# Moving each output store ahead of the round's second load, and ending the hand-written section behind the last store instead of ahead of it

## The chip, the cores and the metric

The kernel runs on one core of one Trainium2 chip. The metric is device time in microseconds (us) of one execution. Before the change the median of three executions is 262.35 us (262.20 to 262.47).

## The reference

For each of 16 batches it multiplies the transpose of a 768 x 512 matrix by a 768 x 1024 matrix, all float32 in memory:

```python
batch, m, k, n = 16, 512, 768, 1024
x: (batch, k, m)   y: (batch, k, n)
np.einsum('bkm,bkn->bmn', x, y).astype(np.float32)
```

So x(b) is 1.5 MB, y(b) 3 MB and the result of a batch 2 MB. Loads and stores together are 109 MB.

## The kernel before

One batch is one round. Everything is written inside one hand-written section (`tc.tile_critical()`, lines 45 and 46): each engine gets a fixed list of instructions, and all waits between engines are semaphores set by hand. The scheduler of the Tile layer orders nothing in it.

- **SP** issues all transfers, on one queue. Lines 102 to 111 are its main loop: for batch b the load of x(b) into `xs[b % 2]` (line 106), the load of y(b) into `ys[b % 2]` (line 109), and, from b = 4 on (`LAG = 4`), the store of the batch four rounds back, `store(b - 4)` (lines 110 and 111, 93 to 100). Below, s(b) is the store of batch b. Ahead of x(b) SP waits until x(b-2) has been cast, and ahead of y(b) until y(b-2) has been cast, because the two float32 buffers of each input are reused every second round. Ahead of s(b), for b below 14, it waits for the `groups` semaphore to reach 2(b+2), which means that TensorE has ended batch b+1; by then ScalarE must have copied batch b out. s(14) waits for `outs`, which ScalarE raises behind its copy of batch 14. After the loop come s(12), s(13) and s(14) (lines 112 and 113).
- **VectorE** casts x(b) and y(b) to bf16, into `xb` and `yb`, two buffers each (lines 118 to 128). Before batch b it waits until TensorE has ended batch b-2. The cast of y(15) alone is cut in two halves.
- **GpSimd** turns finished casts into the semaphore `ready` for TensorE (lines 131 to 134).
- **TensorE** runs 48 matmuls a batch in two groups of 24 (lines 139 to 155); each group fills one half of PSUM and raises `groups`.
- **ScalarE** copies each group from PSUM to one of five output buffers `ob[b % 5]` (lines 161 to 172). Before batch b it waits until s(b-5) has landed.

The end: SP waits until s(11), s(12) and s(13) have landed (lines 174 and 175), and the section is closed (line 176). Closing has a step in which SP signals the four other engines, each answers, and SP waits for all answers. Behind it, in the hands of Tile, stands s(15) (line 181); Tile makes the end of the program wait for its landing and ends with barriers over all engines (they carry the line of the launch, 207).

All transfers lie on one queue, q1, and each is spread over 16 DMA engines; a DMA's semaphore gets 16 landing events, one from each. The order on the queue before the change, in the middle of the run, is x(b), y(b), s(b-4), x(b+1), y(b+1), s(b-3), and so on. At the end it is x(15), y(15), s(11), s(12), s(13), s(14), s(15).

Of the kernel before, what the change touches and what calls it, by code (L numbers as in the profile page):

```python
# [1 line left out]

_os.environ.setdefault("NEURON_RT_ULTRASERVER_MODE", "4")

# [2 lines left out]

# [5 lines left out]


@with_exitstack
def kernel(
    ctx: ExitStack,
    tc: tile.TileContext,
    x: bass.AP,
    y: bass.AP,  # L20
    out: bass.AP,
):
    nc = tc.nc
    P = 128
    FP32 = mybir.dt.float32
    BF16 = mybir.dt.bfloat16

    B, K, M = x.shape
    _, _, N = y.shape
    KT = K // P  # L30
    MT = M // P
    NF = 512
    NT = N // NF

    x_v = x.rearrange("b (p ko) m -> b p ko m", ko=KT)
    y_v = y.rearrange("b (p ko) n -> b p ko n", ko=KT)
    o_v = out.rearrange("b (p mo) n -> b p mo n", mo=MT)

    LAG = 4
    NO = 5
    KH = KT // 2

    section = ExitStack()
    section.enter_context(tc.tile_critical())
    ec = ctx.enter_context
    xs = [ec(nc.sbuf_tensor(f"xs{i}", [P, KT, M], FP32)) for i in range(2)]
    ys = [ec(nc.sbuf_tensor(f"ys{i}", [P, KT, N], FP32)) for i in range(2)]
    xb = ec(nc.sbuf_tensor("xb", [P, 2, KT, M], BF16))  # L50
    yb = ec(nc.sbuf_tensor("yb", [P, 2, KT, N], BF16))
    ob = [ec(nc.sbuf_tensor(f"ob{i}", [P, MT, N], FP32)) for i in range(NO)]

    HB = MT // 2
    ps = [ec(nc.psum_tensor(f"ps{i}", [P, HB, NT, NF], FP32)) for i in range(2)]
    sx = [ec(nc.semaphore(f"sx{i}")) for i in range(2)]
    sy = [ec(nc.semaphore(f"sy{i}")) for i in range(2)]
    so = [ec(nc.semaphore(f"so{i}")) for i in range(NO)]
    cast = ec(nc.semaphore("cast"))
    ready = ec(nc.semaphore("ready"))  # L60
    room = ec(nc.semaphore("room"))
    groups = ec(nc.semaphore("groups"))
    idle = ec(nc.semaphore("idle"))
    outs = ec(nc.semaphore("outs"))


    made = {}

    def wide_dma(key, dst, src, dram_rows, load):


        if key not in made:
            made[key] = nc.sync.dma_start(dst, src)
            return made[key]
        pat = mybir.BassSymbolicTensorAccessPattern
        widen = lambda a: a.rearrange("(q r) k m -> q (r k m)", r=dram_rows)
        plain = lambda a: a.rearrange("p k m -> p (k m)")
        s, d = (widen(src), plain(dst)) if load else (plain(src), widen(dst))
        return nc.sync.add_instruction(_copy.replace(
            made[key].ins, name=nc.get_next_instruction_name(),  # L80
            ins=(pat(ap=s.ap, dtype=s.dtype, bass_ap=s, is_dma=False),),
            outs=(pat(ap=d.ap, dtype=d.dtype, bass_ap=d, is_dma=False),),
            sync_info=None, ant_dge_precooked=False))


    def parts(b):
        return 2 if b in (15,) else 1


    nx = [sum(1 + parts(a) for a in range(b)) + 1 for b in range(B)]  # L90


    def store(b):


        if b < B - 2:
            nc.sync.wait_ge(groups, 2 * (b + 2))
        else:
            nc.sync.wait_ge(outs, b - (B - 3))
        nc.sync.dma_start(o_v[b], ob[b % NO][:]).then_inc(so[b % NO], 16)  # L100

    for b in range(B):
        i = b % 2
        if b >= 2:
            nc.sync.wait_ge(cast, nx[b - 2])
        wide_dma("x", xs[i][:], x_v[b], 4, True).then_inc(sx[i], 16)
        if b >= 2:
            nc.sync.wait_ge(cast, nx[b - 2] + parts(b - 2))
        wide_dma("y", ys[i][:], y_v[b], 2, True).then_inc(sy[i], 16)
        if b >= LAG:  # L110
            store(b - LAG)
    for b in range(B - LAG, B - 1):
        store(b)


    for _ in range(60):
        nc.vector.sem_inc(idle, 1)
    for b in range(B):
        i = b % 2
        n = 16 * (b // 2 + 1)  # L120
        if b >= 2:
            nc.vector.wait_ge(groups, 2 * (b - 1))
        nc.vector.wait_ge(sx[i], n)
        nc.vector.tensor_copy(xb[:, i], xs[i][:]).then_inc(cast, 1)  # L124
        nc.vector.wait_ge(sy[i], n)
        for h in range(parts(b)):
            ks = slice(h * KT // parts(b), (h + 1) * KT // parts(b))
            nc.vector.tensor_copy(yb[:, i, ks], ys[i][:, ks]).then_inc(cast, 1)  # L128


    for b in range(B):
        nc.gpsimd.wait_ge(cast, nx[b]).then_inc(ready, 1)
        for h in range(parts(b)):
            nc.gpsimd.wait_ge(cast, nx[b] + h + 1).then_inc(ready, 2 // parts(b))


    x_w = xb[:].rearrange("p s k (j mo) -> p s k mo j", mo=MT)
    pe = OrderedEngineSet([nc.tensor.engine])
    with nc.Fori(0, B // 2, engines=pe):
        with nc.Fori(0, 2, engines=pe) as s:  # L140
            nc.tensor.wait_ge(ready, 2).then_inc(ready, -2)
            for mo in range(MT):
                g, m = divmod(mo, HB)
                if m == 0:
                    nc.tensor.wait_ge(room, 1).then_inc(room, -1)  # L145
                for kt in range(KT):
                    if mo == 0 and kt == KH:
                        nc.tensor.wait_ge(ready, 1).then_inc(ready, -1)
                    for nt in range(NT):
                        mm = nc.tensor.matmul(  # L150
                            ps[g][:, m, nt], x_w[:, bass.ds(s, 1), kt, mo],
                            yb[:, bass.ds(s, 1), kt, nt * NF:(nt + 1) * NF],
                            start=(kt == 0), stop=(kt == KT - 1))
                if m == HB - 1:
                    mm.then_inc(groups, 1)


    nc.scalar.nop().then_inc(room, 2)
    for _ in range(60):
        nc.scalar.sem_inc(idle, 1)  # L160
    for b in range(B):
        if b >= NO:
            nc.scalar.wait_ge(so[b % NO], 16 * (b // NO))
        for g in range(2):
            nc.scalar.wait_ge(groups, 2 * b + g + 1)
            cp = nc.scalar.copy(ob[b % NO][:, g * HB:(g + 1) * HB].rearrange("p m (t f) -> p m t f", f=NF),  # L166
                                ps[g][:])
            if b < B - 1:
                cp.then_inc(room, 1)
        if b == B - 2:  # L170
            nc.scalar.drain().then_inc(outs, 1)
    cp.then_inc(outs, 1)

    for b in range(B - LAG - 1, B - 2):
        nc.sync.wait_ge(so[b % NO], 16 * (b // NO + 1))
    section.close()

    nc.sync.dma_start(o_v[B - 1], ob[(B - 1) % NO][:])


# [1 line left out]
_INS = ['x', 'y']  # L185
_OUTS = [((16, 512, 1024), 'float32')]


# [23 lines left out]
```

## Time and profile before

| what | value |
|---|---|
| median of three executions | 262.35 us |
| the profiled execution, its own time | 262.47 us |
| its span in the profile | 260.7 us |
| busy: TensorE matmul / VectorE / ScalarE | 186.1 / 82.0 / 61.1 us |
| read from and written to HBM | 75.50 MB, 33.55 MB |
| load of x: count, size, median issue to landing | 16, 1536 KB, 29.7 us |
| load of y | 16, 3072 KB, 28.2 us |
| store | 16, 2048 KB, 32.6 us |

The span runs from the first to the last instruction that the profile counts; the execution's own time is 1.8 us longer. "Landing" is the time from the issue of a DMA to its last landing event, so a transfer that stands long in the queue has a long one. In the views of waits, "SPq" is the instruction stream of SP. In the timelines the columns are: start, duration (both us), engine, line, operation, output and input, count, and in brackets how long the engine had been idle and what ended that.

### The profile page before, as it was taken

How to read it: one execution, taken by the hardware profiler on the slowest of the kernel's cores; microseconds unless marked ns; L12 is line 12 of the kernel's file. 1: busy time of each engine (PE TensorE's matmuls, PEld its weight loads, DVE VectorE, ACT ScalarE, POOL GpSimd, SP SyncE). 2: the span in 40 equal slices, each digit the busy share in tenths (PEclk: the TensorE clock that was granted, in tenths of full speed). 3: DMA queues.
4: the chain of work that ended last, by engine and by line, in shares of the span. 5: the costliest groups of instructions: out<-in, count | busy, mean ns of one | idle time of the engine just before them, and what ended most of it. 6: DMA issues, size and time to landing. Idle time of an engine off the chain costs nothing. (4 is left out here: it accounts for less than half of the span.)

```text
span 260.7 us, 2506 instructions
## 1 busy us (share of the span) xinstructions
PE 186.1 (71%) x768; PEld 89.8 (34%) x768; DVE 82.0 (31%) x33; ACT 61.1 (23%) x33; POOL 0.2 (0%) x4
## 2 busy tenths in 40 slices
PE   0009999998937949479596894969959197696910
PEld 0004555554512515124242351434425043253500
DVE  0261644525222252312524115252142522225000
ACT  1000442243220222202214022040322205022220
POOL 0000000000000000000000000000000000000000
PEclk9999999999995999959889797797999889799985
DMA  7998999999899899989999989999998999999994
GB/s 260 432 494 385 468 385 468 392 392 488 385 410 493 370 450 475 427 385 405 483 400 437 465 367 453 410 483 402 410 485 382 445 468 417 410 410 430 427 410 181
DMA packets 4514, 109.07 MB, mean 418 GB/s; under 512 B 768, under 2 KB 768, under 8 KB 768
## 3 DMA queue, kind: packets, MB, share of 16 engines
q1 hardware_dynamic: 4512, 109.05, 98.1%
q14 instruction: 2, 0.02, 0.0%
HBM read 75.50 MB, written 33.55 MB: 418 GB/s over the span
## 5 line engine op out<-in xcount | busy, mean ns | idle before, releaser
L150 PE MATMUL ps<-yb,xb 128*128 x768 | 186.1, 407 | 62.7 <-PEq L145 60.7
L150 PEld LDWEIGHTS ps<-yb,xb 128*128 x768 | 89.8, 117 | 158.5 <-issue 92.2
L166 ACT COPY ob<-ps 128x2048 f32<-128x2048 f32 x32 | 59.8, 1870 | 184.2 <-PE ps L150 184.2
L128 DVE CAST yb<-ys 128x6144 bf16<-128x6144 f32 (+1 forms) x17 | 53.8, 3171 | 87.7 <-DMA ys<-in_y_dram 87.7
L124 DVE CAST xb<-xs 128x3072 bf16<-128x3072 f32 x16 | 28.2, 1760 | 69.4 <-DMA xs<-in_x_dram 65.3
L166 ACT ACT_TABLE_LOAD x1 | 1.3, 1283 | 5.3 <-issue 5.3
L196 POOL MEMSET const-bfloat16-1.0<- 128x1 bf16 x1 | 0.1, 102 | 0.0
L196 POOL MEMSET const-uint8-127<- 128x1 uint8 x1 | 0.1, 102 | 0.0
L196 POOL MEMSET const-float32-1.0<- 128x1 f32 x1 | 0.1, 99 | 0.0
L196 POOL MEMSET const-float32-0.0<- 128x1 f32 x1 | 0.1, 98 | 0.2 <-issue 0.2
## 6 DMA issues: line engine op xcount, KB each, us to landing
ys<-in_y_dram SPq DMA_DIRECT2D x16, 3072.0 KB, 28.2
out_dram<-ob SPq DMA_DIRECT2D x16, 2048.0 KB, 32.6
xs<-in_x_dram SPq DMA_DIRECT2D x16, 1536.0 KB, 29.7
```

The costliest lines, as they stand in the source:

```text
L124: nc.vector.tensor_copy(xb[:, i], xs[i][:]).then_inc(cast, 1)
L128: nc.vector.tensor_copy(yb[:, i, ks], ys[i][:, ks]).then_inc(cast, 1)
L150: mm = nc.tensor.matmul(ps[g][:, m, nt], x_w[:, bass.ds(s, 1), kt, mo], yb[:, bass.ds(s, 1), kt, nt * NF:(nt + 1) * NF], start=(kt == 0), ...
L166: cp = nc.scalar.copy(ob[b % NO][:, g * HB:(g + 1) * HB].rearrange("p m (t f) -> p m t f", f=NF), ps[g][:])
L196: nc = _bacc.Bacc("TRN2", target_bir_lowering=False, num_devices=1)
```

## The change

Two things are edited; the computation, the transfers' sizes and the buffers stay as they are.

1. For b = 4 to 14 the store s(b-4) is issued between x(b) and y(b), and no longer behind y(b). For b = 15 it stays behind y(15). The loop behind issues s(12) to s(15), s(15) with a wait for `outs` to reach 2, which ScalarE raises with its last copy.
2. The section is entered for the whole function, so that it ends when the function returns. s(15) is inside it, and SP waits inside it for all stores (the five `so` semaphores). Tile issues nothing behind it.

```diff
-    section = ExitStack()
-    section.enter_context(tc.tile_critical())
+    ctx.enter_context(tc.tile_critical())
...
         wide_dma("x", xs[i][:], x_v[b], 4, True).then_inc(sx[i], 16)
+        if LAG <= b < B - 1:
+            store(b - LAG)
         if b >= 2:
             nc.sync.wait_ge(cast, nx[b - 2] + parts(b - 2))
         wide_dma("y", ys[i][:], y_v[b], 2, True).then_inc(sy[i], 16)
-        if b >= LAG:
+        if b == B - 1:
             store(b - LAG)
-    for b in range(B - LAG, B - 1):
+    for b in range(B - LAG, B):
         store(b)
...
-    for b in range(B - LAG - 1, B - 2):
-        nc.sync.wait_ge(so[b % NO], 16 * (b // NO + 1))
-    section.close()
-
-
-
-
-    nc.sync.dma_start(o_v[B - 1], ob[(B - 1) % NO][:])
+    for i in range(NO):
+        nc.sync.wait_ge(so[i], 16 * len(range(i, B, NO)))
```

## The prediction

> **What bounds the kernel now.** I read the DMA rows of the page first.
>
> ```profile
> DMA  7998999999899899989999989999998999999994
> ...
> q1 hardware_dynamic: 4512, 109.05, 98.1%
> ...
> HBM read 75.50 MB, written 33.55 MB: 418 GB/s over the span
> ```
>
> The first row is the busy share of the 16 DMA engines in 40 slices: close to full from the second slice to the last but one. The queue is busy for 98.1% of the span, while TensorE has 71%. The transfers are the bound. Next comes the question whether the queue ever runs dry, which the instruction streams answer. This is one round of the timeline (140 to 176 us).
>
> ```profile
> 140.69 3.36 DVE L128 CAST yb<-ys 128x6144 bf16<-128x6144 f32 x1 [5.45 <-DMA ys<-in_y_dram]
> 140.99 1.87 ACT L166 COPY ob<-ps 128x2048 f32<-128x2048 f32 x1 [3.25 <-PE ps L150]
> 144.08 0.47 SPq L73 DMA_DIRECT2D ys<-in_y_dram  x1
> ...
> 144.58 12.23 PE L150 MATMUL ps<-yb,xb 128*128 x48 [3.63 <-PEq L145]
> 144.59 0.58 SPq L100 DMA_DIRECT2D out_dram<-ob  x1
> ...
> 149.28 1.76 DVE L124 CAST xb<-xs 128x3072 bf16<-128x3072 f32 x1 [5.23 <-DMA xs<-in_x_dram]
> ...
> 151.07 0.47 SPq L73 DMA_DIRECT2D xs<-in_x_dram  x1
> ```
>
> y(9) has landed and is cast at 140.69 to 144.05; then SP issues y(11), and s(7) half a microsecond later; after the cast of x(10) it issues x(12). VectorE and TensorE sit idle until data land, and the page's median landing times are 28 to 33 us for transfers that take 4 to 7 us each. So some 24 us of work stands in the queue at any time. Last, the end:
>
> ```profile
> 219.89 3.36 DVE L128 CAST yb<-ys 128x6144 bf16<-128x6144 f32 x1 [5.46 <-DMA ys<-in_y_dram]
> 223.82 12.24 PE L150 MATMUL ps<-yb,xb 128*128 x48 [4.01 <-PEq L145]
> 235.70 3.43 DVE L128 CAST yb<-ys 128x3072 bf16<-128x3072 f32 x2 [5.46 <-DMA ys<-in_y_dram]
> 238.03 10.72 PE L150 MATMUL ps<-yb,xb 128*128 x48 [1.97 <-ACT ob L166]
> 248.79 1.87 ACT L166 COPY ob<-ps 128x2048 f32<-128x2048 f32 x1 [3.26 <-PE ps L150]
> 250.88 0.33 SPq L181 DMA_DIRECT2D out_dram<-ob  x1
> ```
>
> Batch 14 is cast at 219.89 and multiplied from 223.82, batch 15 from 238.03; its copy ends at 250.66 and s(15) is issued at 250.88. The landing events in the trace show who is last: the 16 engines end s(14) between 251.56 and 255.09, and s(15) between 256.97 and 259.90. One engine lags, and its steps from store to store are 4.85, 4.84, 4.85, 4.81 us for s(12) to s(15): no gap. **The end is this one engine's total of bytes**, not the compute chain: it took s(15) up at 255.09, 4.2 us after the issue.
>
> **The change, part by part.**
>
> *The moved stores, SP's side.* Eleven stores (s(0) to s(10)) change places with eleven loads; no DMA is added. s(b-4) waits until TensorE has ended batch b-3. For b = 11 that is batch 8, at 140.95; x(11) was issued at 135.27, y(11) at 144.08. So the store can go at 141.0, before y(11) may be issued anyway (cast of y(9) ends at 144.05). Behind the waiting store stands y(b), then x(b+1). If TensorE is late, y(b) is late too, but its turn on the queue comes some 20 us after its issue, which hides any such delay. I cost SP's side at nothing; without that cover it would be the store's issue, about 0.5 us a round.
>
> *The moved stores, the queue's side.* On the lagging engine a load of x takes 3.66 us, of y 7.28, a store 4.86: 15.8 a round in either order. y(4) to y(14) land 4.86 us later and the store 7.28 earlier; x stays. All are needed later than they land but y, and a later y moves VectorE and TensorE alike by 4.9 us. Steady state: y lands, 3.4 us cast, 0.5 to the first matmul, 10.5 to 13.5 of matmuls, within 15.8. Nothing ends on this before the tail, so 0.
>
> *The queue's losses at transitions.* 16 times 15.8 is 252.8 us; from the first packet at 1.98 that gives 254.8, and the lagging engine ends at 259.90. Of the 5.1 us lost, 2.2 are the first two loads (5.26 and 7.93 us); 2.4 are four loads, y(4), y(5), y(6) and y(8), with steps of 7.84, 8.01, 7.93 and 7.76 instead of 7.28. In the packet records the late packets are those that stand last before a store: 1.82 us normally, up to 2.63 there. Before a load they are not late. After the change the last packet of x stands before the store, of the same 49152 bytes, and the number of such transitions is 12 as before (s(11) still follows y(15)). The trace doesn't show x before a store: the bounds are that all these losses go (2.5 us less) and that each of the 12 transitions costs the largest excess seen, 0.8 us (9.7 less 2.5, 7 us more). I take 0, since packet, size and count are the same and the steps after y(10) show hardly any loss.
>
> *The tail, compute.* y(14) now lands at 224.73, when s(10) landed before, and not at 219.87. Its matmuls start 3.95 us after that, at 228.68; with 12.24 us they end at 240.92. Batch 15 waits for them instead of for its data (ready at 237.6), and back to back a batch takes 10.36 (starts of 31.36 and 41.72 in the early part, where TensorE runs without idle time). That gives 251.28, the copy ends at 253.2, and s(15) is issued at about 253.25 instead of 250.88. Before, the middle engine landed s(15) 6.2 us after its issue (257.08 less 250.88), so now at 259.45. The lagging engine starts s(15) at 255.09 in either case and ends at 259.90. So it still ends last, by 0.45 us: cost 0, cover 0.45 us. A DMA's fixed cost as the Trainium skill gives it bears on this: "DMA: Bandwidth & Descriptors", section "Anatomy of one DMA — SWDGE (gpsimd) path", puts it at about 2.0 us plus bytes over 436 GB/s, though for another way of issuing than this kernel's. An estimate from that page is 6.8 us for a store, so landing at 260.05 and 0.15 us lost; the trace's 6.2 us decides here.
>
> *The end of the section.* Before, its closing lies ahead of s(15): by the records SP sees s(13) landed at 250.25, signals at 250.48, the engines answer to 250.70, SP has all answers at 250.79 and issues s(15) at 250.88. That is 0.63 us, beside the lagging engine's transfer of s(13) and s(14), so it cost nothing. After the last landing (259.90) came 0.07 us of SP's wait and then the final barriers to 260.70. Now the same closing comes behind the last landing, with nothing beside it, and then the same final barriers: **+0.63, less about 0.05** for Tile's own wait for s(15), which goes. The nearest row is the closing itself, so I take 0.58. The bounds are 0.3 (the signal at 250.48 to the issue, if the 0.23 before it is not repeated) and 0.8 (two more semaphores to be waited for).
>
> *Sum:* 0 + 0 + 0 + 0 + 0.58. The profiled execution has 262.47, which becomes 263.05. It lies 0.12 above the median of the runs shown, so I forecast 262.35 + 0.6 = **262.95 us**, 0.23% slower. About 0.2%, or 0.5 us, is what a measurement of this kernel can tell from no change.
>
> **The rivals.**
>
> *The compute tail ends last.* If TensorE's first matmuls of batch 14 run at the half clock for longer, s(15) comes too late to be hidden. For it: of the batches from 5 on, two took 13.51 and 13.37 us instead of 12.24, with a granted clock of 0.5 for 6.8 us. That is 1.2 more, less the cover of 0.45: 0.75 more, 263.7. It decides once s(15) is issued later than 253.7. Against: the batches 4, 6 and 12 took 10.55. Chance 0.20, 263.1 to 264.0.
>
> *Fewer losses at the transitions, so faster.* If what makes the last packet late is tied to y (its 24 KB for each partition, or the moment in the round at which it lands), an x before the store is spared. Price: 2.5 us on the lagging engine at most, from y(4), y(5), y(6), y(8) and y(10); with the 0.6 of the end, 260.45; at half, 261.7. It decides when more than 0.6 of the 2.5 goes. For it: seven of the twelve transitions cost nearly nothing, so the loss depends on something. Against: x packets are as large. Chance 0.22, 260.4 to 262.6.
>
> *More losses at the transitions.* Casts of y now run when x's last packets land, which they didn't. One to two us more on top of 0.6: 264 to 265. Chance 0.08.
>
> *It doesn't do what it says.* The closing could overlap the last landings, or the landing of the lagging engine could vary by that much: 262.2 to 262.7, chance 0.05.
>
> **How the numbers follow.** The forecast, 262.6 to 263.3 with the bounds of the closing, has 0.45; of that 0.30 lie above 262.87 (0.2%) and 0.15 below. Slower: 0.30 + 0.20 + 0.08 = 0.58. Faster: 0.17 of the second rival's 0.22. Within 0.2%: 0.15 + 0.05 + 0.05 = 0.25. The range 261.3 to 264.0 leaves out the far half of the faster rival (0.08) and most of the third (0.06).
>
> **What would show it.** Right: q1's busy time (98.1% of 260.7, 255.7 us) is the same; the last landing stays within 0.4 us of 259.9; the time from it to the end of the span grows from 0.8 to 1.4 us; s(15) is issued near 253.3; TensorE starts batch 15 without idle time. Wrong: a last landing earlier by a microsecond with fewer late packets (second rival), a last landing 6.2 us behind the issue of s(15) (first rival), or slices with the DMA below 9 in the middle, which would mean that the queue does run dry.

## The result

The changed kernel takes 263.20 us (median of four, 263.03 to 263.59), the kernel before, run beside it, 262.27 us (median of four, 261.99 to 262.47). The ratio is 1.0038, with a 95% interval of 1.0021 to 1.0056: slower by 1.0 us, 0.55 to 1.5. The forecast was 262.95 us, 0.23% slower. The changed kernel's profiled execution has 263.36 us and a span of 261.6 (before: 262.47 and 260.7).

The DMA rows of the changed kernel's page:

```profile
DMA  6998999999999999989999998999999999999994
...
q1 hardware_dynamic: 4512, 109.05, 97.9%
...
HBM read 75.50 MB, written 33.55 MB: 417 GB/s over the span
```

The queue is as full as before: 97.9% of 261.6 is 256.1 us of packet time, against 255.7. No slice between the first and the last falls below 8, and three have 8, where the kernel before has six. The transfers still are the bound. One round of its timeline (129 to 152 us):

```profile
129.90 3.36 DVE L129 CAST yb<-ys 128x6144 bf16<-128x6144 f32 x1 [10.31 <-DMA ys<-in_y_dram]
130.18 0.34 SPq L99 DMA_DIRECT2D out_dram<-ob  x1
...
133.29 0.47 SPq L72 DMA_DIRECT2D ys<-in_y_dram  x1
133.66 1.76 DVE L125 CAST xb<-xs 128x3072 bf16<-128x3072 f32 x1 [0.40 <-DMA xs<-in_x_dram]
133.79 12.23 PE L151 MATMUL ps<-yb,xb 128*128 x48 [3.64 <-PEq L146]
135.45 0.47 SPq L72 DMA_DIRECT2D xs<-in_x_dram  x1
```

The store goes out at 130.18, as soon as TensorE has ended the batch that it waits for, and the load of y at 133.29, when the cast ends. SP's waits for TensorE grew from 28.2 to 130.2 us, and its waits for the casts of y shrank from 117.0 to 57.3 (total, count and longest, the first two lines before the change, the others after it):

```profile
SPq L73 <- DVE yb L128: 117.0, 14, 9.1
SPq L100 <- PE ps L150: 28.2, 4, 15.9
...
SPq L99 <- PE ps L151: 130.2, 13, 13.9
SPq L72 <- DVE yb L129: 57.3, 12, 13.2
```

That is one wait turned into another. x now lands right behind y, so that VectorE casts both in a row (0.40 us idle between them) and then idles 10.3 us in one piece. The end:

```profile
229.11 20.91 PE L151 MATMUL ps<-yb,xb 128*128 x96 [3.74 <-PEq L146]
...
236.15 3.43 DVE L129 CAST yb<-ys 128x3072 bf16<-128x3072 f32 x2 [5.46 <-DMA ys<-in_y_dram]
...
250.06 1.87 ACT L167 COPY ob<-ps 128x2048 f32<-128x2048 f32 x1 [3.26 <-PE ps L151]
```

Batch 14 starts at 229.11 and batch 15 follows without idle time (one row of 96 matmuls). s(15) is issued at 251.95. Its landing events run from 258.05 to 260.36, and the span ends at 261.59. So the 0.9 us of span come from two places: the last landing is 0.46 later (260.36, not 259.90), and from there to the end are 1.23 us instead of 0.79, 0.44 more.

For each kernel below I give two readings of its trace beside its time. "Loss of the lagging engine" is what the latest of the 16 landing events of each DMA took beyond 3.66, 7.28 and 4.86 us for x, y and a store, summed over all DMAs behind the first y: 2.87 us in the kernel before, 3.49 in the changed one. "Late packets" is the time that the last load packets ahead of a store took beyond 1.84 us, summed over the 16 engines. The packet records don't name the engine; packets are put to engines by their times, so a sum over many changes is good to about half a microsecond.

### The profile page after: what moved, and what is told of

It reads as the page before. It is cut to its first block, busy times and chain, and to the rows that moved or that the text cites. A ratio compares the mean times of both kernels' runs of the same rounds, so it can differ in the third digit from the quotient of the medians.

```text
span 261.6 us, 2506 instructions
## 1 busy us (share of the span) xinstructions
PE 190.3 (73%) x768; PEld 90.5 (35%) x768; DVE 82.0 (31%) x33; ACT 61.1 (23%) x33; POOL 0.2 (0%) x4
## 3 DMA queue, kind: packets, MB, share of 16 engines
q1 hardware_dynamic: 4512, 109.05, 97.9%
## 5 line engine op out<-in xcount | busy, mean ns | idle before, releaser
L151 PE MATMUL ps<-yb,xb 128*128 x768 | 190.3, 414 | 59.8 <-PEq L146 59.7
L125 DVE CAST xb<-xs 128x3072 bf16<-128x3072 f32 x16 | 28.2, 1760 | 18.0 <-DMA xs<-in_x_dram 15.0
## 6 DMA issues: line engine op xcount, KB each, us to landing
ys<-in_y_dram SPq DMA_DIRECT2D x16, 3072.0 KB, 28.2
```

What stands on the lines that cost most here:

```text
L151: mm = nc.tensor.matmul(ps[g][:, m, nt], x_w[:, bass.ds(s, 1), kt, mo], yb[:, bass.ds(s, 1), kt, nt * NF:(nt + 1) * NF], start=(kt == 0), ...
```

## The experiments

**1. The moved stores alone**, with the section closed ahead of the last store as before.

```diff
+        if LAG <= b < B - 1:
+            store(b - LAG)
...
-        if b >= LAG:
+        if b == B - 1:
             store(b - LAG)
```

> The moved stores alone; the section ends ahead of the last store, as before the change. My theory (part of the 0.9 us is the closing of the section behind the last landing, 0.45 by the two traces; the rest is late packets at the change from load to store, 0.5): 0.3 to 0.7 us slower than before, with 3 us lost on the lagging engine at the transitions. Rival (the order is neutral and all of the 0.9 is the closing and its waits): 0 within 0.2. Rival (the order is all of it): 0.9.

Measured: 262.85 us (six executions, 262.04 to 263.51) against 262.06; ratio 1.0034 (1.0019 to 1.0049), 0.9 us slower. The lagging engine's loss is 3.37 us, 1.09 of it at x(4), the first load ahead of a store; from the last landing (260.22) to the end are 0.79 us as before. This speaks for a part of the cost in the order. But a spread of 1.5 us over six executions made me measure it again (run 12).

**2. The new end alone**, the stores behind y.

```diff
-    section = ExitStack()
-    section.enter_context(tc.tile_critical())
+    ctx.enter_context(tc.tile_critical())
...
-    for b in range(B - LAG, B - 1):
+    for b in range(B - LAG, B):
         store(b)
...
-    section.close()
...
-    nc.sync.dma_start(o_v[B - 1], ob[(B - 1) % NO][:])
+    for i in range(NO):
+        nc.sync.wait_ge(so[i], 16 * len(range(i, B, NO)))
```

> The new end alone; the stores stay behind y. My theory: 0.45 us slower, all of it between the last landing and the end of the span (1.2 us there instead of 0.8). Rival (the closing is hidden or costs nothing): 0. Rival (the end is all of it): 0.9.

Measured: 262.56 us (262.49 to 262.61) against 262.06; ratio 1.0023 (1.0010 to 1.0036), 0.26 to 0.94 us slower. The lagging engine's loss is 2.72 us, like the kernel before, and 1.23 us lie between the last landing (259.54) and the end of the span. That is 0.44 us more than before, and no other loss. By time alone all of the 0.9 us lies just inside the interval; the trace decides for 0.44.

**3. Stores in pairs behind y** of every odd round, half as many changes from loads to stores.

```diff
-        if b >= LAG:
+        if b > LAG and b % 2:
+            store(b - LAG - 1)
             store(b - LAG)
```

> The end as before the change; the stores go in pairs, s(b-5) and s(b-4) behind y(b) of every odd round, so the queue changes from loads to stores 6 times instead of 12. If each such change costs something (2.5 us on the lagging engine in all before): about 1.2 us faster. If only the first few changes cost, or the loss is independent of their number: within 0.5 us. If the later stores hold ScalarE up, slower.

Measured: 261.48 us (261.39 to 261.56) against 262.06; ratio 0.9982 (0.9969 to 0.9994), 0.5 us faster. The late packets are 4.0 us at the first change (68.6 us) and 0.5 us in all at the five others; the kernel before has 6.4 at its first and 8.7 at its others. The lagging engine's loss is 2.26 us. The gain is less than half of what a fixed cost for each change would give, so this left open whether their number counts.

**4. Stores cut in two by partitions**, one half between x and y, one behind y.

```diff
+            q = slice(h * P // 2, (h + 1) * P // 2)
+            nc.sync.dma_start(o_v[b, q], ob[b % NO][q]).then_inc(so[b % NO], 16)
```

> The end as before the change; each store is cut in two by partitions (its packets keep 16384 bytes), one half between x and y and one behind y, so the queue changes from loads to stores 23 times instead of 12. If each change costs about 0.2 us on the lagging engine: 2 to 3 us slower than before. If the loss doesn't follow the number of changes: within 0.7 us of the order-alone kernel.

Measured: 276.42 us (271.77 to 281.52), ratio 1.045 (1.041 to 1.050), 14 us slower. That is no test of the number of changes, since the halves themselves cost more than the change. Two rows of its page:

```profile
DMA  7999999999999999999999999999999999999982
GB/s 260 445 445 452 402 431 438 383 368 409 440 356 414 359 426 428 407 378 409 397 433 419 459 397 438 416 445 416 440 433 440 423 426 438 419 390 332 311 297 105
```

The engines are busy to the end, but in the last slices, where only stores run, they move 390 to 297 GB/s instead of 410 to 430. A store packet of 16384 bytes that takes 0.61 us takes up to 2.55 there. That is the smaller part of the 13.3 us by which this profile's span is longer: y(15) lands at 243.57, 7.9 us later than before the change, and 5.3 us are lost behind it. The 7.9 us are all lost in rounds 4 to 9; from round 10 to the last load a round takes 15.8 us, as in the kernel before, though the halves stay. So it isn't simply that stores over 64 partitions are slow, and why they were slow in two stretches was not tried. The question about the number of changes went to runs 6 and 7.

**5. Pairs ahead of y**, as run 3, but between x(b) and y(b).

```diff
+        if LAG < b < B - 1 and b % 2:
+            store(b - LAG - 1)
+            store(b - LAG)
...
-        if b >= LAG:
+        if b == B - 1:
+            store(b - LAG - 1)
             store(b - LAG)
```

> Pairs of stores as in the pairs kernel, but between x(b) and y(b) of the odd rounds 5 to 13 and behind y(15). Six changes from loads to stores, five of them behind x. If x ahead of a store costs more than y (the late packets of the first change sum to 14 us over the 16 engines behind x(4), and to 7 to 8 behind y(4)): the first change, at x(5), again about 14 us of late packets, where the pairs kernel had 4.2 at y(5), and 0.3 to 0.6 us slower than the pairs kernel. If the sum only falls with the time of the first change: about 5 us of late packets and the pairs kernel's time within 0.2.

Measured: 261.60 us (twelve executions, 261.47 to 261.86) against 262.24; ratio 0.9974 (0.9965 to 0.9983), 0.7 us faster. The late packets are 4.9 us at x(5) and 1.3 at the five others, the lagging engine's loss 2.05. In pairs, an x ahead of a store is no worse than a y: my reading that x costs more falls. This kernel beats the one before and the changed one.

**6 and 7. Stores cut in two by rows**, all 128 partitions in each half, packets of 8192 bytes. In run 6 both halves stand behind y, in run 7 one stands between x and y.

```diff
+            q = slice(h * HB, (h + 1) * HB)
+            nc.sync.dma_start(o_v[b][:, q], ob[b % NO][:, q]).then_inc(so[b % NO], 16)
```

> The kernel before, with each store except the last cut in two by output rows of a partition (8192-byte packets, all 128 partitions), both halves behind y. 12 changes from loads to stores. A control for the next kernel: it shows what smaller packets cost. With a fixed cost for each packet, 0 to 3 us slower than before.

> The same halves, one between x and y and one behind y: 23 changes from loads to stores. If each change costs on the lagging engine (2.6 to 2.8 us for 12, most of it in the first five): 1 to 3 us slower than the control. If the number of changes doesn't matter: within 0.5 us of the control plus the 0.8 of the moved order.

Measured: together 262.78 us (262.48 to 262.96), ratio 1.0018 (1.0008 to 1.0029); apart 261.74 us (261.54 to 262.17), ratio 0.9985 (0.9975 to 0.9995), both against 262.24. With 23 changes the kernel is 1.0 us faster than with 12 of the same packets. In run 7 the late packets are 13.7 us at the first change (x(4)) and 1.1 in all at the 22 others; in run 6 they are 11.9 and 7.9. The lagging engine's loss is 2.25 us in run 7 and 3.46 in run 6. **A fixed cost for each change from loads to stores is refuted.** Why run 7 is the faster one stays open.

**8. The changed kernel with a late last store**: two more copies of the last group ahead of its own, into buffers that nobody reads any more.

```diff
+            if b == B - 1 and g == 1:
+                nc.scalar.copy(xs[0][:, :4], ps[g][:].rearrange("p m t f -> p (m t) f"))
+                nc.scalar.copy(ys[0][:, :2].rearrange("p a (t f) -> p a t f", f=NF), ps[g][:])
```

> The changed kernel, with two more copies of the last group from PSUM ahead of its own (into buffers that nobody reads), so that the last store is issued 3.74 us later, at 255.7. By the cover that the prediction named (the last store may be issued up to 6.2 us before the lagging engine's end, 254.2 in the changed kernel's trace): all engines then wait for the store, it lands 6.1 to 6.3 us behind its issue, and the time is 1.4 to 1.9 us above the changed kernel's. If the queue hides it all the same: 0.

Measured: 265.70 us (264.46 to 266.18) against 262.24; ratio 1.0119 (1.0087 to 1.0150). That is 2.1 us above the changed kernel by the ratios. Its timeline:

```profile
251.14 1.87 ACT L168 COPY xs<-ps 128x2048 f32<-128x2048 f32 x1 [3.26 <-PE ps L151]
252.90 1.87 ACT L169 COPY ys<-ps 128x2048 f32<-128x2048 f32 x1
254.66 1.88 ACT L170 COPY ob<-ps 128x2048 f32<-128x2048 f32 x1
256.57 0.33 SPq L99 DMA_DIRECT2D out_dram<-ob  x1
```

and its stretches, with the DMA share in the last column but one:

```profile
252.00:256.00 4.00, 0.00 (x0) 0.00 (x0) 0.00 (x0) 4.00 (x3) 0.00 (x0) 0.98 0.11 45
256.00:260.00 4.00, 0.00 (x0) 0.00 (x0) 0.00 (x0) 0.54 (x1) 0.00 (x0) 0.50 0.76 319
```

The queue was all but dry from 252 to 256 (0.11 busy). s(15) landed on all engines between 262.68 and 262.83, 6.1 to 6.3 us behind its issue. So the cover ends where the prediction put it, and past it a late copy costs its full time: the lagging engine, which ended s(14) at 254.92, would have ended s(15) at 259.78, and 256.57 + 6.2 is 3.0 us later; it measured 3.04 more than a store's 4.86. The store came 0.9 us later than I expected, mostly because batch 14 took 12.2 us here and 10.6 in the changed kernel's profile; that is also why the cost lies above the 1.4 to 1.9 us expected.

**9 and 10. The moved order in two halves**: run 9 leaves s(0) behind y(4) and moves s(1) to s(10); run 10 moves s(0) alone. Both have the end of the kernel before.

```diff
+        if LAG < b < B - 1:        # run 9;   run 10: if b == LAG
+            store(b - LAG)
...
-        if b >= LAG:
+        if b in (LAG, B - 1):      # run 9;   run 10: if b > LAG
             store(b - LAG)
```

> The moved stores with the end as before the change, but s(0) stays behind y(4); s(1) to s(10) go between x and y. By now the number of changes from loads to stores is no cause (the kernel with 23 was faster than its control), and the first change alone is late on all 16 engines in every run (12 to 14 us in sum behind x(4), 6 to 12 behind y(4), 4 to 5 in round 5). If the moved order costs by this first change: the order-alone kernel's 0.8 us shrinks to 0 to 0.3. If it costs by the later rounds or by the compute tail: 0.6 to 0.9 stay.

> The kernel before, with s(0) alone moved between x(4) and y(4). If the first change is the cause: 0.4 to 0.8 us slower than before, with 12 us of late packets or more at 50 us. If the later rounds are: 0 within 0.2. The compute tail is that of the kernel before in this one, so nothing of the time can come from there.

Measured, both against 262.25: run 9 262.19 us (twelve, 261.57 to 263.58), ratio 1.0005 (0.9991 to 1.0019); run 10 262.36 us (261.84 to 262.92), ratio 1.0004 (0.9994 to 1.0014). Run 10 has late packets of 10.8 us at its first change, on all 16 engines, and no measurable loss of time: of these, 0.50 us fell on the lagging engine. That the first change behind x(4) is the cause falls as well. The two halves sum to 0.2 us, not to the 0.9 of run 1, though their intervals reach up to 0.5 and 0.4 us.

**11. One pair, then singles**: no store in round 4, s(0) and s(1) behind y(5), one store behind each y after that.

```diff
-        if b >= LAG:
+        if b == LAG + 1:
+            store(b - LAG - 1)
+        if b > LAG:
             store(b - LAG)
```

> The kernel before, with no store in round 4 and both s(0) and s(1) behind y(5); from round 6 on one store behind each y. If the pairs kernel's gain of 0.6 us is the later first change alone (4 us of late packets instead of 6 to 8): 0.3 to 0.6 us faster than before. If it needs the pairs in all rounds: within 0.2.

Measured: 262.22 us (twelve, 261.41 to 262.98) against 262.25; ratio 0.9990 (0.9980 to 1.0001). The late packets are 3.0 us at the first change and 9.6 at the eleven others. A later first change gives 0 to 0.5 us, so it is at most a part of what pairs in all rounds give (0.4 to 0.9 in run 5).

**12. The moved order once more**, run 1's kernel.

> The order-alone kernel once more: its six executions lay between 262.0 and 263.5, while the order without the first store, and the first store alone, each measured 0.1 us. If the two halves add up (0.1 + 0.1) and the first measurement was high: 0 to 0.4 us slower than before. If the moved order costs 0.8 only as a whole: 0.6 to 1.0 again. In either case the trace should show the lagging engine ending 0 to 0.5 us later than in the kernel before, and the last store issued near 253.

Measured: 262.49 us (twelve, 261.88 to 263.12) against 262.13; ratio 1.0012 (1.0000 to 1.0024), 0.3 us slower. So the two halves add up within the intervals, and run 1 read high; the intervals of the two runs meet at 0.5 to 0.6 us. The two were made on different chips, each beside the kernel before, so a difference between chips isn't excluded. The trace also shows something that run 1 had not shown. From its timeline:

```profile
228.04 23.61 PE L152 MATMUL ps<-yb,xb 128*128 x96 [3.96 <-PEq L147]
...
251.69 1.86 ACT L168 COPY ob<-ps 128x2048 f32<-128x2048 f32 x1 [3.26 <-PE ps L152]
253.75 0.33 SPq L183 DMA_DIRECT2D out_dram<-ob  x1
```

and its stretches:

```profile
250.00:253.00 3.00, 1.66 (x8) 0.66 (x6) 0.00 (x0) 1.31 (x1) 0.00 (x0) 1.00 0.73 311
253.00:256.00 3.00, 0.00 (x0) 0.00 (x0) 0.00 (x0) 0.56 (x1) 0.00 (x0) 0.68 0.66 279
```

Batches 14 and 15 take 23.61 us together, where the changed kernel's profile has 20.91. s(15) is issued at 253.75, and the engines idle a third of 253 to 256 (0.66 busy). The lagging engine ended s(14) at 254.47, but its s(15) took 5.59 us instead of 4.86, and all engines landed it between 259.85 and 260.06, 6.1 to 6.3 us behind the issue. In this execution the compute tail ended last: the first rival, at a price of 0.73 us (0.75 in the prediction). Its condition, an issue later than 253.7, was only just met. Runs 1 and 9 lay close to it: they issued s(15) at 253.66 and 252.97, and the lagging engine ended only 0.34 and 0.43 us behind the middle ones.

## Why the prediction was right

- **What bounds the kernel**: right. The queue has 256.1 us of packet time in the changed kernel and 255.7 before, and the end is the lagging engine's chain (258.05 for the first engine, 260.36 for the last).
- **SP's side, taken as nothing**: right. SP's waits for TensorE grew by 102 us, and the queue did not notice: transfers landed a median of 24 to 30 us behind their issue there, so more than a round of work stood in it.
- **A later y, taken as nothing before the tail**: right. The DMA share (last column but one) is 1.00 from 57 to 232 us in both kernels, before and after:

```profile
57.00:232.00 175.00, 133.44 (x537) 63.11 (x535) 56.32 (x22) 42.13 (x23) 0.00 (x0) 0.89 1.00 428
57.00:232.00 175.00, 134.25 (x520) 61.90 (x518) 56.33 (x22) 41.09 (x22) 0.00 (x0) 0.86 1.00 429
```

One reading was loose: 3.4 + 0.5 + 13.5 is 17.4 us, not within 15.8. It does no harm, because VectorE casts the next y while TensorE multiplies; what has to fit in 15.8 is each engine's own part, 13.5 at most.
- **Losses at the transitions, taken as 0**: mis-sized. In the two profiles the lagging engine loses 3.49 us instead of 2.87, 0.62 more, and one change, at x(4), costs it 1.18, more than the 0.8 taken as the largest. The third rival (more losses) had the sign and a price that was too high. The moved order in all costs 0.5 to 1.3 us by run 1 and 0 to 0.6 by run 12. The count of changes, on which I rested the 0, doesn't set these losses: 23 changes lost less than 12 (runs 7 and 6). Nor does x ahead of a store in place of y (run 5), and late packets on all engines need not cost time (run 10). What makes a packet late stays open. Nor is it settled how the order's cost divides between late packets and the compute tail, since single profiles of one kernel differ by as much: runs 1 and 12 have 13.7 and 6.9 us of late packets at x(4), and losses of 3.37 us with no wait for s(15) and of 3.22 us with 0.73 of it.
- **The compute tail, cover 0.45 us**: right in its mechanism. Batch 14 started at 229.11 (228.68 predicted), batch 15 followed without idle time, and the first engine landed s(15) 6.1 us behind its issue. Where batch 14 took the 12.2 us of the prediction, in the profiles of runs 1 and 9, the cover was 0.34 and 0.43 us. In the profiled execution it took 10.55 us, so the cover was 2.3 us, which is luck; in run 12 it took 13.3, and there was none. The Trainium skill's 2.0 us plus bytes over 436 GB/s ("DMA: Bandwidth & Descriptors", section "Anatomy of one DMA — SWDGE (gpsimd) path") would give an estimate of 6.8 us for this store; runs 8 and 12 measure 6.1 to 6.3, so this queue's own row was the better one to take.
- **The closing, +0.58**: measured +0.44, inside the bounds of 0.3 to 0.8, and 0.6 (0.26 to 0.94) by time in run 2. In the records of the changed kernel it runs from 260.37 (SP sees s(15) landed) to 260.87, 0.50 us and not 0.63; less about 0.06 for Tile's own wait, that is the 0.44. From SP's signal to the last answer it is 0.30 us (260.53 to 260.83), as before (250.48 to 250.79, 0.31), though ScalarE's answer took 0.01 us instead of 0.17. What didn't come again is one more wait of SP ahead of the signal (0.07) and 0.05 of the 0.09 us between the last answer and the next instruction. The mechanism was right, the term 0.14 too large.
- **The sum**: 0.58 predicted against 1.0 (0.55 to 1.5). The closing gave 0.44; the rest, by difference, is the moved order, which I had taken at 0. So the forecast came close with one term a little too large and another left out.
- **The second rival, faster by 0.6 to 1.9 us**, did not come in this change. But its idea, that the losses can be avoided, did: pairs of stores are 0.7 us faster (run 5).
- **The signs**: batch 15 without idle time and the longer time behind the last landing (1.23 us, 1.4 forecast) came. The last landing moved by 0.46 us, a little more than the 0.4 allowed, and s(15) went out 1.35 us ahead of 253.3. DMA digits below 9 in the middle were no sign at all: the kernel before has six of them in the row that the prediction shows.

## What to carry to other kernels

In this kernel one queue is full from start to end. There the order of whole transfers moved the time by tenths of a microsecond, while a serial step behind the last landing counted in full: put a handshake ahead of the last transfer, where the queue hides it. Ask of a reordering what becomes late at the end, and give the slack as a time (here: the last store costs nothing if it is issued at least 6.2 us ahead of the slowest engine's end), and hold it against the slowest duration that any round of the trace shows, not against the usual one: here 10.55 and 13.3 us of the same batch lay on either side of it.

## What the runs showed of the hardware

- The 16 DMA engines of one queue drift apart: by 0.9 to 1.4 us after the first two loads, by 2.1 to 3.9 us at s(14) in all runs but run 4, and only the last counts (in the kernel before, s(14) lands between 251.56 and 255.09).
- The last load packets ahead of the first store were late on 11 to 16 of the engines in every run: by 3 to 14 us in sum, less in round 5 (3 to 5) than in round 4 (6.8 to 14 at x(4), 6 to 12 at y(4)).
- With stores over 64 partitions instead of 128, and packets of the same size, the kernel was 14 us slower (run 4). Behind the last load a store packet took up to 2.55 us instead of 0.61; in rounds 10 to 15 a round took no longer than before.
- Behind a pause, the same matmuls of one batch took 10.55 to 10.7 us, 11.8 to 12.9 or 13.1 to 13.5, with none, 2.6 to 4.8 or 5.1 to 6.05 us of them at a granted clock of 0.5. In all the traces together, pauses of 2.3 to 3.1 us gave the middle one (26 of 26), pauses of 3.1 to 4.05 us gave all three (11, 24 and 25 times), and longer ones never the first (49). The half-clock stretches in the clock records, up to the last matmul, are 3.41 or 6.83 us long, or 10.24 around pauses of more than 8 us. The Trainium skill ("TensorE: Matmul & The Clock Gate", section "Part 1: The HAM clock gate") has a window of about 3.4 us that runs free of the kernel; these lengths, one, two or three windows, agree with it, and so does the fact that pauses of one length ended in three ways.
